# Linear attention in a streaming encoder layer: one 128-column product per decay level for two chunks, outputs with tokens as rows

## The chip, the cores and the metric

The kernel runs on one core of a Trainium2 chip. A core has five engines with a queue of instructions each: PE (matrix products, with its weight loads shown apart as PEld), DVE and ACT (elementwise work), POOL and SP (here mostly issuers of transfers). Each engine works its own queue in order; semaphores make one engine wait for another. Products land in PSUM, a store of eight banks of 512 fp32 columns by 128 partitions; everything else is in SBUF or in DRAM. The metric is the device time of one execution in microseconds (us), and the figure for the kernel before is the median of three runs.

## The reference

One layer of a hybrid encoder for 1024 prompt tokens and 32 sample tokens. The part that the change touches is branch A, a gated linear recurrence with four heads (128 key and 256 value channels per head). Cut to that:

```python
log_a = jax.nn.log_sigmoid((alr @ w_a2 + b_a2).astype(f32)) / GATE_TAU
qb = to_blocks(q, DK_A) * DK_A ** -0.5          # kb, vb, ab likewise

def step(S, inp):
    qi, ki, vi, ai = inp
    b = jnp.cumsum(ai, axis=2)
    decay = jnp.exp(jnp.where(mask, b[:, :, :, None, :] - b[:, :, None, :, :], -jnp.inf))
    scores = jnp.einsum('bhic,bhjc,bhijc->bhij', qi, ki, decay)
    o = (jnp.einsum('bhij,bhjv->bhiv', scores, vi)
         + jnp.einsum('bhic,bhcv->bhiv', qi * jnp.exp(b), S))
    bl = b[:, :, -1]
    S = (jnp.exp(bl)[..., None] * S
         + jnp.einsum('bhjc,bhjv->bhcv', ki * jnp.exp(bl[:, :, None] - b), vi))
    return S, o

s_fin, o = lax.scan(step, s0.astype(f32), (qb, kb, vb, ab))
o = o * lax.rsqrt(jnp.mean(o * o, axis=-1, keepdims=True) + EPS)
o = o.reshape(B, T, V_A) * g_gla.astype(f32)
o = o.astype(q.dtype) * jax.nn.silu(r)
```

Around it stand the input projection `h @ w_in`, a band softmax attention (branch B), the two output projections, a gated convolution feed-forward and an embedding gate, all with normalisations.

## The kernel before

Channels are partitions and tokens are columns through most of the kernel. Dense products run at a precision better than one pass by splitting each operand into a rounded high part and a low remainder (`hi`, `lo`) and adding three products.

The work is staged: input projections, the band attention, the linear attention, the output projections, then the feed-forward and the gate. In the band and linear stages, which are made of small dependent steps, the kernel weaves in dense input projections: `piece()` puts a third of one projection unit on PE (9, 9 or 6 matmuls of 352 columns, lines 808 to 810), `flush()` puts the evacuation of finished units on ACT. The number of units is fixed. PE, DVE and ACT run in the order in which the code issues their instructions (`manual_schedule`); POOL and SP, which issue the transfers, are ordered by the scheduler.

The linear attention takes a head in four segments of 256 tokens (the last has the 32 sample tokens as well, 288 columns), two chunks of 128 tokens each. The main loop `for u in range(16)` does one segment per iteration, head `u // 4`, segment `u % 4`, and prepares the next one beside it.

The decay between two tokens is a product over channels, so the scores cannot be one matrix product. They are built by levels. For level l, with m = 2 to the power l, each block of 2m tokens takes the running sum b of the log gates at its middle as reference: `differences` (DVE, line 1181) subtracts it, `exponentials` (ACT, lines 1201 and 1202; level 6 and the end-of-chunk factors from `refs`, 1190 to 1196) makes decays, `factors` (DVE, 1215, 1209) multiplies the first half of the block by the keys and the second half by the queries, in the same tile `x`. A product of `x` with itself then holds, for that level, the scores between first and second half. `level_products` makes for each of the two chunks and each of levels 1 to 6 one product with the chunk as stationary operand and the 64 second-half columns as moving operand (1242); the diagonal (1227) and level 0 (1233, with `qo`) are made from keys and queries. `score_copies` (DVE, 1264 and 1268) picks the valid elements with byte masks from PSUM into `scores`, which has keys as partitions. `key_turns` and `key_copies` transpose the decayed keys (PE 1249, ACT 1254: tile `kt`), `updates` makes the new states (PE 1283, DVE 1293).

`outputs` makes the output with value channels as partitions, two halves by two chunks, values and state as stationary operand (1306, 1308). For the norm, `squares_a` copies, squares and adds (ACT 1334, 1338, DVE 1340), splits the sum into two parts (1342, 1343), and `sums_a` sums over partitions with a matrix of ones (PE 1348, 1349), so that each partition has the sum of every token. `roots` (ACT 1355 to 1357) and, in the next iteration, `results` (DVE 1365 to 1368) make the inverse root and apply it with the silu gate `sr`.

`decays(h + 1)` is the preparation of the next head in steps: the gate projection (1054), absolute value, exponential and logarithm on ACT (the last is 1060), nine scans on DVE (1064) that give b, the references, and `qo` (1079 to 1082). The loop takes 5, 4 and 3 steps in segments 0, 1 and 2. PSUM has two banks for dense products (`mm`), four single ones (`one`) and one pair (`two`) here.

Of the kernel before, what the change touches and what calls it, by code (L numbers as in the profile page):

```python
# [17 lines left out]
P = 128  # L18
# [95 lines left out]
def emit(tc, a):  # L114
# [584 lines left out]
    masks = tl(gc, [P, 7, 64], U8, tag="masks")  # L699
# [30 lines left out]
    def head_tiles(h):  # L730
        def row(i, scale):
            return lambda ps, s: ac.activation(HA[h][i][:, s], ps, AF.Copy, scale=scale)

        def store(i):
            return lambda t: dma.dma_start(d_kq[i], t)

        box, scale = lambda: HA.setdefault(h, {}), float(P ** -0.5)
        if h:
            kq = [(K0 + h, row("k", 1.0)), (Q0 + h, row("q", scale))]
        else:  # L740
            kq = [(K0 + h, mover(box, "k", 1.0, store(0))), (Q0 + h, mover(box, "q", scale, store(1)))]
# [98 lines left out]
    def band_constants():  # L840
# [8 lines left out]
        for l in range(7):  # L849
            yield  # L850
            m = 1 << l
            po.memset(mf[:, l], 1.0)
            v = mf[:, l].rearrange("p (n m) -> p n m", m=m)
            pat = [[-2 * m, 64 // m], [0, m]]
            po.affine_select(out=v, in_=v, pattern=pat, compare_op=ALU.is_ge, fill=0.0, base=0, channel_multiplier=1)
            pat = [[2 * m, 64 // m], [0, m]]
            po.affine_select(out=v, in_=v, pattern=pat, compare_op=ALU.is_ge, fill=0.0, base=m - 1, channel_multiplier=-1)
        yield
        ve.tensor_copy(masks, mf)
# [183 lines left out]
    def decays(h):  # L1043
        g = HA[h]
        b = g["b"] = tl(gp, [P, T], tag="b", bufs=2) if h else evt()
        ub = b
# [30 lines left out]
        bo, qo = blocks(b, 1), tl(gp, [P, T // 2], tag="qo", bufs=1)  # L1077
# [60 lines left out]
    next(end)  # L1138
    bp.release()

# [3 lines left out]
    scores = [tl(gp, [P, 2, P], tag=f"scores{i}") for i in range(2)]  # L1144
    scores_s = tl(gp, [NS, NS], tag="scores_s")
    for t in scores:
# [25 lines left out]
    def differences(u, ls):  # L1172
# [5 lines left out]
        for l in ls:  # L1178
            m, w = 1 << l, level_width(l, nt)
            bv = blocks(b[:, t0 : t0 + w], m)  # L1180
            ve.tensor_tensor(blocks(x[:, l - 1, :w], m), bv, bv[:, :, m - 1 : m].to_broadcast([P, w // (2 * m), 2 * m]), op=ALU.subtract)

    def exponentials(u, ls):
        g, h, s, t0, nt = seg(u)
        x = X[u]
        for l in ls:
            if l == 7:
                for o in range(0, nt, P):
                    n, w = (t0 + o) // P, min(P, nt - o)
                    ac.activation(x[:, 6, o : o + w], g["b"][:, t0 + o : t0 + o + w], AF.Exp, scale=1.0 / TAU, bias=g["refs"][:, n : n + 1])  # L1190
                ac.activation(x[:, 7, :nt], g["b"][:, t0 : t0 + nt], AF.Exp, scale=-1.0 / TAU)
                continue
            if l == 6:
                for o in range(0, 256, 64):
                    up_, n = o // 64 % 2, (t0 + o) // P
                    ac.activation(x[:, 5, o : o + 64], g["b"][:, t0 + o : t0 + o + 64], AF.Exp, scale=(-1.0 if up_ else 1.0) / TAU,
# [1520 lines left out]
```

## Time and profile before

| | |
|---|---|
| median of 3 runs | 1938.35 us (1938.24 to 1938.88) |
| the profiled execution, its own time | 1942.58 us |
| its span, first to last instruction | 1940.9 us |
| granted PE clock, mean over the span | 0.996 |
| linear attention | about 599 to 912 us of the span |

Each row of a timeline has a start (us from the span's start), a duration in us, the engine, the line, the operation, output tile `<-` inputs, the shape, and how many records are merged. In brackets stands the idle time of the engine before it and what ended it. One fp32 product on PE shows as two records, a transpose or a product of rounded operands as one. Durations on PE overlap their neighbours; the distance between starts does not.

### The profile page before, as it was taken

To read this page: it belongs to the slowest core of one execution; us is meant where nothing else is said; L and a number is where in the kernel's file an instruction comes from. 1 tells how busy PE (TensorE), PEld (TensorE's weight loads), DVE (VectorE), ACT (ScalarE), POOL (GpSimd) and SP (SyncE) were. 2 spreads that over 40 slices of the span, in tenths; PEclk is the share of its full clock that TensorE was granted. 3 is DMA by queue.
4 is the path that set the end of the run, shared out by engine and by line. 5 is a ranking of instruction groups with operands and counts; after the bars stand their busy time and mean duration, and the time that the engine had idled before them with its cause. 6 is when DMAs were issued, how large, how long until landed. Compare 5 with 4: busy or idle time off the path is not lost.

```text
span 1940.9 us, 34940 instructions
## 1 busy us (share of the span) xinstructions
PE 1896.0 (98%) x13960; PEld 1862.0 (96%) x13960; DVE 1258.7 (65%) x2287; ACT 959.0 (49%) x1919; POOL 210.2 (11%) x352
## 2 busy tenths in 40 slices
PE   8999999999999999999999999999999999999996
PEld 8999998998999999999999999999999999999996
DVE  6955544555556776777444685877767766558776
ACT  7544334666666565554233444433334344555555
POOL 0000000000000101001220111111111211000112
PEclk9999999999999999999999999999999999999998
DMA  7223335233315555667844346444354558897746
GB/s 274 85 95 122 100 96 165 74 87 90 93 48 146 142 133 157 166 181 224 299 134 128 105 159 221 159 150 150 113 126 111 124 144 292 273 295 241 242 149 107
DMA packets 111118, 300.91 MB, mean 155 GB/s; under 512 B 12452, under 2 KB 34796, under 8 KB 110316
## 3 DMA queue, kind: packets, MB, share of 16 engines
q1 hardware_dynamic: 81500, 205.95, 33.8%
q0 software_dynamic: 28016, 88.05, 16.9%
q10 hardware_dynamic: 1440, 4.69, 0.6%
q8 instruction: 109, 1.79, 0.4%
q14 instruction: 53, 0.43, 0.1%
HBM read 201.20 MB, written 114.09 MB: 162 GB/s over the span
## 4 chain that ended last, share of the span: by engine, by line
PE 75%; DVE 11%; ACT 7%; DMA 3%; issue 2%; ACTq 0%; SPq 0%; DVEq 0%
PE mm L230 6%; PE mm L232 6%; PE mm L231 6%; PE two L1931 6%; PE two L1932 6%; PE two L1933 6%; PE mm L808 4%; PE two L618 4%; PE two L619 4%; PE two L620 4%; PE mm L810 3%; PE mm L809 3%; PE two L2393 2%; PE two L2392 2%; PE two L2391 2%
## 5 line engine op out<-in xcount | busy, mean ns | idle before, releaser
L808 PE MATMUL mm<-xh,whi 128*128 128x352 f32 x696 | 236.8, 340 | 2.5 <-ACT ev L714 1.8
L810 PE MATMUL mm<-xh,wlo 128*128 128x352 f32 x696 | 225.4, 324 | 0.0
L809 PE MATMUL mm<-xl,whi 128*128 128x352 f32 x696 | 224.6, 323 | 0.0
L2393 PE MATMUL two<-d,wlo 128*128 128x264 f32 x616 | 175.5, 285 | 0.5 <-DVE wlo L2130 0.5
L2392 PE MATMUL two<-d,whi 128*128 128x264 f32 x616 | 174.7, 284 | 0.8 <-DVE d L2081 0.8
L2391 PE MATMUL two<-d,whi 128*128 128x264 f32 x616 | 174.7, 284 | 0.2 <-ACT whi L2129 0.2
L1933 PE MATMUL two<-mh,wlo 128*128 128x264 f32 x576 | 163.3, 285 | 0.2 <-DVE wlo L1922 0.2
L1932 PE MATMUL two<-ml,whi 128*128 128x264 f32 x576 | 162.9, 284 | 0.0
L1931 PE MATMUL two<-mh,whi 128*128 128x264 f32 x576 | 161.4, 285 | 1.5 <-DVE gx L1943 1.5
L808 PEld LDWEIGHTS mm<-xh,whi 128*128 128x128 f32 x696 | 131.3, 189 | 5.0 <-ACT ev L714 2.1
L809 PEld LDWEIGHTS mm<-xl,whi 128*128 128x128 f32 x696 | 131.3, 189 | 0.4
L810 PEld LDWEIGHTS mm<-xh,wlo 128*128 128x128 f32 x696 | 130.5, 188 | 0.0
L2392 PEld LDWEIGHTS two<-d,whi 128*128 128x128 f32 x616 | 115.9, 188 | 1.2 <-DVE d L2081 1.2
L2391 PEld LDWEIGHTS two<-d,whi 128*128 128x128 f32 x616 | 116.5, 189 | 0.5 <-ACT whi L2129 0.5
L2393 PEld LDWEIGHTS two<-d,wlo 128*128 128x128 f32 x616 | 115.5, 188 | 0.9 <-DVE wlo L2130 0.9
L1931 PEld LDWEIGHTS two<-mh,whi 128*128 128x128 f32 x576 | 107.3, 188 | 1.7 <-DVE gx L1943 1.7
L1933 PEld LDWEIGHTS two<-mh,wlo 128*128 128x128 f32 x576 | 108.5, 188 | 0.4 <-DVE wlo L1922 0.4
L1932 PEld LDWEIGHTS two<-ml,whi 128*128 128x128 f32 x576 | 108.4, 188 | 0.0
L944 ACT ACTIVATE s<-s,sm 128x640 f32<-128x640 f32 (+5 forms) x72 | 50.8, 705 | 97.9 <-DVE sm L943 97.9
L619 PE MATMUL two<-tl,whi 128*128 128x264 f32 x320 | 90.8, 284 | 0.0
L618 PE MATMUL two<-th,whi 128*128 128x264 f32 x320 | 90.8, 284 | 0.0
L620 PE MATMUL two<-th,wlo 128*128 128x264 f32 x320 | 90.6, 284 | 0.0
(620 smaller groups left out, 5959.6 us busy)
## 6 DMA issues: line engine op xcount, KB each, us to landing
raw<-in_w_in SPq DMA_DIRECT2D x52, 512.0 KB, 3.7
d_b<-av POOLq DMA_DIRECT2D x33, 528.0 KB, 4.0
d_ws<-in_w_down POOLq DMA_DIRECT2D x24, 704.0 KB, 6.6
uraw<-d_b SPq DMA_DIRECT2D x32, 528.0 KB, 5.2
raw<-in_w_up SPq DMA_DIRECT2D x27, 512.0 KB, 3.6
wraw<-d_ws SPq DMA_DIRECT2D x16, 704.0 KB, 6.4
d_b<-gc POOLq DMA_DIRECT2D x11, 792.0 KB, 6.1
sraw<-in_w_up SPq DMA_DIRECT2D x17, 512.0 KB, 4.6
```

The costliest lines, as they stand in the source:

```text
L618: pe.matmul(ps[:, j, :HC], w[0][:, k], x[0](k, s), start=st, stop=False, skip_group_check=True)
L619: pe.matmul(ps[:, j, :HC], w[0][:, k], x[1](k, s), start=False, stop=False, skip_group_check=True)
L620: pe.matmul(ps[:, j, :HC], w[1][:, k], x[0](k, s), start=False, stop=sp_, skip_group_check=True)
L808: pe.matmul(ps, wh, h[:, k, s], start=(k == 0), stop=False)
L809: pe.matmul(ps, wh, l[:, k, s], start=False, stop=False)
L810: pe.matmul(ps, wl, h[:, k, s], start=False, stop=(k == cnt - 1))
L1931: pe.matmul(ps[:, j, :HC], w[0][:, k], x[0][:, k, s], start=st, stop=False, skip_group_check=True)
L1932: pe.matmul(ps[:, j, :HC], w[0][:, k], x[1][:, k, s], start=False, stop=False, skip_group_check=True)
L1933: pe.matmul(ps[:, j, :HC], w[1][:, k], x[0][:, k, s], start=False, stop=sp_, skip_group_check=True)
L2391: pe.matmul(o, wh, xh_[:, s], start=(k == 0 and p in (0, 4, 5)), stop=False, skip_group_check=True)
L2392: pe.matmul(o, wh, xl_[:, s], start=False, stop=False, skip_group_check=True)
L2393: pe.matmul(o, wl, xh_[:, s], start=False, stop=(k == HD - 1 and p in (3, 4, 6)), skip_group_check=True)
```

## The change

The queries are stored with the two chunks of a pair swapped, in `kq` (`row_swapped`, and four transfers in place of one for head 0), and `decays` makes a second copy of b with the chunks swapped likewise (`both`). `differences` and `factors` then leave in `x` for each level, in the first 128 columns, keys of the first chunk's first halves between queries of the other chunk's second halves, and the reverse in the other 128 columns. One product of these two 128-column parts holds the scores of both chunks: one with keys as partitions, the other with queries as partitions, that is transposed. So `level_products` makes one 128-column product per level where there were two of 64 columns.

The scores of one chunk come out transposed in `sc[:, 0]`: the new `score_turn` transposes them on PE, ACT copies them to `turned`, and DVE puts in level 0. The masks get a second set. `score_copies` runs in two parts, the first (diagonal to level 3) between the level products.

`outputs` now has scores and decayed queries as stationary operands and values and state as moving operands of 256 columns, so tokens are partitions. The norm's sum over channels is then a sum along a row: `squares_a` lets ACT square with an accumulated sum, `roots` works on one number per token and scales the outputs on ACT, and the new `output_turns` transposes them back on PE in the next iteration, where `results` multiplies by the gate. The two products with ones are gone. In PSUM the stage has two `mm` and six `one` banks; unfinished projection units are completed before the change of layout. `decays` has one step more; the loop takes 5, 4, 2 and, in segment 3, two single steps.

How the instructions stand. First PE, in the iteration for head 1, segment 2, from the first product on; dense matmuls are left out at each line of dots. `kq` holds keys and queries, `x` the factors, `vt` the values with tokens as partitions. Before:

```order
L1227 MATMUL one_8102<-kq_6854 128x128 x2
L1233 MATMUL two_8103<-qo_7417,kq_6854 128x64 x2
L1249 MATMUL one_8108<-ident_78,x_7897 128x128 x2
...
L1242 MATMUL two_8103<-x_7897 128x64 x4
...
L1283 MATMUL one_8136<-vt_6855,kt_8134 128x256 x2
L1242 MATMUL two_8103<-x_7897 128x64 x4
...
L1306 MATMUL one_8222<-scores_1112_6731,vt_6855 128x128
L1308 MATMUL one_8222<-x_7897,state_7937 128x128
```

After:

```order
L1325 MATMUL one_8161<-vt_6900,kt_8159 128x256 x2
L1271 MATMUL one_8129<-x_7922 128x128
L1271 MATMUL one_8130<-x_7922 128x128
L1405 MATMUL one_8175<-ident_78,ot_8071 128x128 x4
...
L1279 MATMUL one_8240<-ident_78,scores_1113_6773 128x128
...
L1348 MATMUL one_8257<-state_7961,x_7922 128x256
L1349 MATMUL one_8257<-vt_6900,scores_1113_6773 128x256
L1348 MATMUL one_8257<-state_8164,x_7922 128x256
L1349 MATMUL one_8257<-vt_6900,turned_6775 128x256
```

Four 64-column products became two of 128; the transposes of the previous segment's outputs and of the scores were put in; the last output product reads `turned`.

Next DVE, in the same iteration, from the state updates to the factors of the next segment (`wlo` is the low part of a projection's weights). Before:

```order
L1293 SCALAR_TENSOR_TENSOR state_8141<-state_8139,be_7409,one_8136 128x256
L1264 COPY_PREDICATED scores_1112_6731<-eye_3247,one_8102 128x256
L1268 COPY_PREDICATED scores_1112_6731<-masks_3246,two_8103 128x128
...
L1268 COPY_PREDICATED scores_1112_6731<-masks_3246,two_8103 128x2x64
L1181 TENSOR_TENSOR x_8097<-b_7007 128x256
L1209 TENSOR_TENSOR x_8097<-x_8097,kq_6854 128x576
L1215 TENSOR_TENSOR x_8097<-x_8097,kq_6854 128x288 x4
```

After:

```order
L1311 COPY_PREDICATED scores_1113_6773<-masks_3246,one_8130 128x2x64
L1416 TENSOR_TENSOR sr_7920<-one_8175,sr_7920 128x2x256
L1206 TENSOR_TENSOR x_8123<-both_7448 128x256
L1235 TENSOR_TENSOR x_8123<-x_8123,kq_6899 128x576
L1241 TENSOR_TENSOR x_8123<-x_8123,kq_6899 128x288 x2
L236 TENSOR_TENSOR wlo_8228<-raw_7840,whi_8227 128x512
L1281 COPY_PREDICATED turned_6775<-masks_3246,one_8129 128x64
L1241 TENSOR_TENSOR x_8123<-x_8123,kq_6899 128x288 x2
```

Behind the last level's copy stand now the previous segment's result, the difference, three factors and a weight split, and then the level-0 copy into `turned`.

Last ACT, from the end of segment 1 of head 1 to the key copy of segment 2 (`ev` is the gate of the next head, `kq` the evacuation of a projection, `kt` the key copy). Before:

```order
L1334 ACTIVATE ot_8041<-one_8032 128x2x256
L1338 ACTIVATE sq_1289_8043<-ot_8041 128x2x256
L1342 ACTIVATE y_1290_8046<-sq_1289_8043 128x256
L1060 ACTIVATE ev_7834<-ev_7834 128x1056
L1162 ACTIVATE vt_6855<-one_8064 32x256
L1355 ACTIVATE sq_1289_8043<-one_8080 128x256
...
L732 ACTIVATE kq_7661<-mm_8009 128x352
L1254 ACTIVATE kt_8134<-one_8108 128x256
```

After:

```order
L1383 ACTIVATE ot_8071,sums_8070<-one_8065 128x256 x2
L1070 ACTIVATE ev_7861<-ev_7861 128x1056
L1186 ACTIVATE vt_6900<-one_8089 32x256
L1391 ACTIVATE y_8105<-sums_8070 128x2
L1392 ACTIVATE y_8105<-y_8105 128x2
L1398 ACTIVATE ot_8071<-one_8065,rs_8108 128x256 x2
L740 ACTIVATE kq_7690<-mm_8040 128x32
L740 ACTIVATE kq_7690<-mm_8040 128x128 x2
L740 ACTIVATE kq_7690<-mm_8040 128x64
L1293 ACTIVATE kt_8159<-one_8135 128x256
```

The scaled copies (L1398), which need DVE's `rs`, stand ahead of the evacuation, now in pieces, and of the key copy.

The core of the diff (masks, the swapped query row, and reads of the copy of b in the exponentials are left out):

```diff
     def decays(h):
+        both = g["b"] = tl(gp, [P, 2, T], tag="both", bufs=1)
+        pairs = ((both[:, 0], b), (to[:, :, 1], of[:, :, 0]), (to[:, :, 0], of[:, :, 1]), (both[:, 1, NP:], b[:, NP:]))
+        for i, (t, f) in enumerate(pairs):
+            if i and not h:
+                ve.tensor_copy(t, f)
+            else:
+                ac.activation(t, f, AF.Copy)
+        yield
...
+    repsum((2, 6, 0))
...
     def level_products(u, between):
         for l in range(1, 7):
+            if l == 4:
+                score_copies(u, range(-1, 4))
             if l % 2:
                 between[l // 2]()
-            m = 1 << l
-            for i, (n, o, w) in enumerate(ns):
-                if 2 * m <= w:
-                    xs = x[:, l - 1, o : o + w]
-                    pe.matmul(to(i, l, w), xs, blocks(xs, m)[:, :, m:], start=True, stop=True)
+            pe.matmul(level_bank(u, l), x[:, l - 1, 0:P], x[:, l - 1, P : 2 * P], start=True, stop=True)
...
+    def score_turn(u):
+        r = R[u]
+        ps = ps_one()[:, :P]
+        pe.transpose(ps, r["sc"][:, 0], ident)
+        ac.activation(turned, ps, AF.Copy)
+        ve.copy_predicated(turned.rearrange("p (n s) -> p n s", s=2)[:, :, 1], masks[:, 0, 1], level_bank(u, 0)[:, 64:128])
...
     def outputs(u):
-            for j in range(2):
-                f, d = slice(j * P, (j + 1) * P), ps[:, j * 256 + i * P : j * 256 + (i + 1) * P]
-                pe.matmul(d, g["vt"][:, n, f], r["sc"][:, i], start=True, stop=(n == 0))
-                if n:
-                    pe.matmul(d, S[h, n - 1][:, f], x[:, 7, o : o + w], start=False, stop=True)
+            if n:
+                pe.matmul(d, x[:, 7, P - P * i : 2 * P - P * i], S[h, n - 1], start=True, stop=False)
+            pe.matmul(d, turned if i else r["sc"][:, 1], g["vt"][:, n], start=(n == 0), stop=True)
...
     def squares_a(u):
+        for w, i, ps in parts:
+            ac.activation(t[:w, i], ps, AF.Square, accum_out=v[:w, i : i + 1])
+        ve.tensor_scalar(v, v, 1.0 / 256, EPS, op0=ALU.mult, op1=ALU.add)
...
     def roots(u):
+        ac.activation(y, r["sums"][:, :n], AF.Ln)
         ac.activation(y, y, AF.Exp, scale=-0.5)
+        ve.scalar_tensor_tensor(v, y, -0.5, v, op0=ALU.mult, op1=ALU.mult)
+        ve.tensor_tensor(v, v, y, op=ALU.mult)
+        ve.scalar_tensor_tensor(rs, v, 1.5, y, op0=ALU.add, op1=ALU.mult)
+        for w, i, ps in parts_of(u):
+            ac.activation(r["t"][:w, i], ps, AF.Copy, scale=rs[:w, i : i + 1])
+
+    def output_turns(u):
+                pe.transpose(ps[:, 256 * j + P * i : 256 * j + P * i + P], r["t"][:, i, P * j : P * j + P], ident)
...
     def results(u):
+        ve.tensor_tensor(o[:, :, :256], r["ot"].rearrange("p (j t) -> p j t", t=256), o[:, :, :256], op=ALU.mult)
...
 for u in range(16):
+        def turn_back():
+            if u:
+                output_turns(u - 1)
+            piece()
+
+        level_products(u, (turns, states, turn_back))
...
-        score_copies(u, range(-1, 7))
+        score_copies(u, range(4, 7))
+        if u:
+            results(u - 1)
...
+            factors(u + 1, (7, 1, 2))
+        steps_of(piece, 2)
+        score_turn(u)
+        if u < 15:
+            factors(u + 1, (3, 4, 6))
             exponentials(u + 1, (5,))
-        steps_of(piece, 3)
+        piece()
...
-        sums_a(u)
         roots(u)
...
+    output_turns(15)
     results(15)
```

180 lines of the change are left out of this document (106 added, 74 removed).

## The prediction

> **What bounds the kernel now.** I read the page's totals first, then the table of busy time for the stretch in which the linear attention runs (597 to 912 us), then the timeline of one of its sixteen iterations, engine by engine.
>
> ```profile
> PE 1896.0 (98%) x13960; PEld 1862.0 (96%) x13960; DVE 1258.7 (65%) x2287; ACT 959.0 (49%) x1919; POOL 210.2 (11%) x352
> ...
> 597.00:912.00 315.00, 311.49 (x2134) 298.72 (x2133) 224.23 (x556) 176.90 (x527) 31.48 (x50) 1.00 0.59 163
> ```
>
> The first row is the whole span with PE busy for 98% of it. The columns of the second are the stretch, its length, and the busy time of PE, PEld, DVE, ACT and POOL, then the granted clock (1.00). PE is idle for 3.5 us of 315; DVE has 29% to spare, ACT 44%. Dense projections fill every hole that the attention leaves on PE, and their number does not change. So in this stretch a microsecond of PE work removed is a microsecond gained, as long as no new wait stands where the old work stood.
>
> The profile's durations overlap on PE, so I price PE work by the distance of starts. This is iteration 6 (head 1, segment 2), PE:
>
> ```profile
> 713.44 0.28 PE L1348 MATMUL one<-y,onesHr 128*128 128x256 f32 x1
> 713.67 0.39 PE L1349 MATMUL one<-y,onesHr 128*128 128x256 f32 x1
> 713.89 0.61 PE L1227 MATMUL one<-kq 128*128 128x128 f32 x4
> 714.34 0.56 PE L1233 MATMUL two<-qo,kq 128*128 128x64 f32 x4
> 714.73 0.39 PE L1249 MATMUL one<-ident,x 128*128 128x128 f32 x2
> 714.87 0.41 PE L808 MATMUL mm<-xh,whi 128*128 128x352 f32 x1
> 715.12 0.32 PE L809 MATMUL mm<-xl,whi 128*128 128x352 f32 x1
> ...
> 716.41 1.00 PE L1242 MATMUL two<-x 128*128 128x64 f32 x8
> 717.22 0.41 PE L808 MATMUL mm<-xh,whi 128*128 128x352 f32 x1
> 717.46 0.33 PE L809 MATMUL mm<-xl,whi 128*128 128x352 f32 x1
> ...
> 718.76 1.03 PE L1283 MATMUL one<-vt,kt 128*128 128x256 f32 x4
> 719.62 1.00 PE L1242 MATMUL two<-x 128*128 128x64 f32 x8
> ...
> 726.28 0.38 PE L1306 MATMUL one<-scores,vt 128*128 128x128 f32 x2
> ...
> 728.23 0.32 PE L809 MATMUL mm<-xl,whi 128*128 128x352 f32 x1
> ```
>
> A dense matmul of 352 columns takes 0.161 us (eight from 715.12 to 716.41). An fp32 product is two records. Two products of 128 columns (four records, L1227) go by in 0.45 us, 0.112 us a record. Four products of 64 columns (eight records, L1242) take 717.46 - 716.41 - 0.16 = 0.89 us up to the second dense matmul: 0.111 a record. So 64 columns cost what 128 cost; something of fixed length, the weight load by the look of it, sets the pace. 256 columns (L1283) cost 0.86 / 4 = 0.215 a record. A transpose (L1249) is one record: (715.12 - 714.73 - 0.16) / 2 = 0.115.
>
> **The change, part by part, on PE, per iteration.** Each line is the work that goes or comes, by these prices.
> - Levels 1 to 6: twelve products of 64 columns become six of 128, twelve records fewer: 12 x 0.112 = 1.34 us less.
> - Outputs: sixteen records of 128 columns (726.28 to 728.23, less 0.16: 1.79) become eight of 256 (8 x 0.215 = 1.72): 0.07 less.
> - The two norm products L1348 and L1349 go. At the dense rate 256 columns are 0.117 each, 0.23 for both; from 713.44 to 713.89 they hold PE for 0.45. I take the middle, 0.34, and keep both ends (16 x 0.11 = 1.8 us either way).
> - Five transposes come (one for the turned scores, four for the outputs): 5 x 0.115 = 0.57 more.
> - Products for the 32 sample tokens change form in four iterations: wider moving operands, fewer instructions. I put them at zero, 0.3 us an iteration either way.
>
> Sum: 1.34 + 0.07 + 0.34 - 0.57 = 1.18 us, over sixteen iterations 18.9 us less PE work. Nothing on PE covers this or is covered by it: it is the path.
>
> The level products hold most of this, and there a rule of the Trainium skill speaks against the change. In "TensorE: Matmul & The Clock Gate", section "Back-to-back issue gap", the gap of an isolated matmul grows with its columns: about 60 cycles up to 64 columns, 134 at 128. By it one product of 128 columns would cost a little more than two of 64, and the 1.34 us would be about nothing. The rows above differ (0.112 against 0.111 a record), and the same section says that weight loads in a stream set a floor, so I go by the rows; the sum by the rule is the last of the rivals.
>
> **What the other engines have to do in time.** The outputs of the second chunk now need a chain that did not exist: last level copied into the scores (DVE), scores turned (PE), moved to SBUF (ACT), level 0 patched in (DVE), then the product. For its length, DVE in the same iteration, and the sample copies of iteration 7:
>
> ```profile
> 714.16 2.75 DVE L1064 TENSOR_TENSOR_SCAN b<-b,ev 128x128 f32<-128x128 f32 x9 [0.22 <-ACT ev L1060]
> ...
> 720.52 0.99 DVE L1293 SCALAR_TENSOR_TENSOR state<-state,be,one 128x256 f32<-128x256 f32 x2
> 721.43 0.44 DVE L1264 COPY_PREDICATED scores<-eye,one 128x256 f32<-128x256 uint8 x1
> 722.52 2.60 DVE L1268 COPY_PREDICATED scores<-masks,two 128x128 f32<-128x128 uint8 x7 [0.65 <-PE two L1242]
> 725.03 0.42 DVE L1181 TENSOR_TENSOR x<-b 128x256 f32<-128x256 f32 x1
> 725.36 0.75 DVE L1209 TENSOR_TENSOR x<-x,kq 128x576 f32<-128x576 f32 x1
> 726.03 1.90 DVE L1215 TENSOR_TENSOR x<-x,kq 128x288 f32<-128x288 f32 x5
> 727.84 0.69 DVE L236 TENSOR_TENSOR wlo<-raw,whi 128x512 fp32r<-128x512 f32 x1
> ...
> 746.37 0.98 DVE L1275 COPY_PREDICATED scores_s<-masks,one 32x16 f32<-32x16 uint8 x5
> ```
>
> PE's new timetable, from the iteration's first product: opening 1.07 (713.89 to 715.12 less 0.16), nine dense 1.45, two levels 0.45, nine dense 1.45, updates 0.86 (ends at 5.3), two levels 0.45, four transposes 0.46, six dense 0.97, two levels 0.45 (level 6 ends at 7.6), eighteen dense 2.90, the turn 0.12 (10.6), six dense 0.97, three output products of 0.43: at 12.9 us the turned scores are wanted.
>
> DVE: states from 5.5 (0.23 us behind PE, as 722.52 is behind the end of the products) for 0.91; diagonal 0.44; level 0, 64 elements wide, 0.25 (between the 0.2 of L1275 and the 0.36 of L1268); three levels at 0.36 (2.51 / 7), to 8.2; three more to 9.3. Then the new result multiply, 512 elements, at 0.67 like L1209: 9.9; difference 0.33, factors 0.67 and 2 x 0.36, weight split 0.6, to 12.3; the level-0 patch 0.25 and 0.1 to 0.2 of signalling: 12.7 against 12.9. It just fits; queued behind the patch are the other factors, which are wanted an iteration later. I allow 0.15 us in each of twelve iterations: 1.8 us. In segment 3 DVE has 1.1 us of sample copies and 0.7 (like L1209) of the next head's qo more ahead of the patch, and starts the last copies 0.9 later, while PE's sample products move the need by 1.3 only: 12.7 + 2.7 = 15.4 against 14.2. Three iterations wait 1.1 us each: 3.3 us. (The sixteenth has no next segment to prepare.)
>
> Next, ACT around the end of segment 1 of head 1:
>
> ```profile
> 710.98 0.60 ACT L1334 ACTIVATE ot<-one 128x512 f32<-128x512 f32 x1 [1.19 <-PE one L1308]
> ...
> 713.06 1.07 ACT L1060 ACTIVATE ev<-ev 128x1056 f32<-128x1056 f32 x1
> ...
> 715.81 0.38 ACT L1254 ACTIVATE kt<-one 128x256 f32<-128x256 f32 x1
> ```
>
> Before, ACT does its part of the norm and goes on to the key copy `kt` at 4.8 us behind its first look at the outputs. Now its scaled copies (L1398 after) wait for three small DVE instructions, and in segment 1 these stand behind the nine scans (2.75 us). ACT: two squares with their sums, no row has that form, between 0.8 (two copies like `kt`) and 1.3 (as much as the copy and the square now gone), I take 1.2; logarithm 1.07; scans 2.75; three small operations 0.5; two scaled copies 0.75; four pieces of the query row instead of one, 1.0; `kt` 0.38: 7.7 us. PE wants `kt` after 2.7 us of fill (fifteen dense matmuls and two transposes) and 4.4 of the next iteration (its opening, nine dense, two levels, nine dense), 7.1. Behind ACT's wait stand the evacuation of a projection bank and `kt`, and PE's update waits for that. Where the fill is longer (segments 0 and 2, up to 24 dense matmuls) it is hidden. I count 1.0 us for the stage. That DVE loses some 2 us of norm arithmetic in each iteration gains nothing by itself: it is not the bound.
>
> The beginning has no slack:
>
> ```profile
> 598.74 0.71 DVE L1082 TENSOR_TENSOR qo<-qo,kq 128x528 f32<-128x528 f32 x1 [6.75 <-DMA kq<-d_kq]
> 598.76 0.52 PEld L1227 LDWEIGHTS one<-kq 128*128 128x128 f32 x4 [0.57 <-ACT vt L1162]
> ```
>
> The first products start the moment `kq` lands. It now comes by four transfers on SP's queue, and ACT's copy of b (1.07, like L1060) goes ahead of the exponentials. Between 0 and 2.5 us; I take 1.0. At the end, the turned outputs of the sixteenth segment stand behind two and a half pieces of dense work, about 3.9 us, and their chain (squares of three parts 1.8, four splits on ACT at the 0.44 of L1264's width 1.8, roots and three scaled copies 2.1) is 5.7: 2 us of wait.
>
> The extra mask building in the band phase is on POOL, idle there, and one more DVE copy; the query row's eleven pieces are 1.7 us of ACT per head with 44% of it free: zero. They lose their cover only if ACT becomes late, which is the point above.
>
> Waits: 1.8 + 3.3 + 1.0 + 1.0 + 2.0 = 9.1 us. Net 18.9 - 9.1 = 9.8 us less: the profiled execution's 1942.58 us would be 1932.8. It stands 4.2 us above the median of the runs, 1938.35, so the median should come to 1928.5; I say 1928.
>
> **Rivals.**
> - No wait shows: DVE and ACT run ahead where I have them just late. The spare 29% and 44% speak for it; the missing slack at the start and the segment-3 sum speak against it. 1938.35 - 18.9 = 1919.5, with the upper end of the norm products 1918.
> - The waits eat the gain: the patch comes 0.65 us later in fifteen iterations than I have it (0.65 x 15 = 9.8), by signalling between four engines for instance. 1938. My margin of 0.2 us speaks for it.
> - Slower: the predicated copies. They now read PSUM with a stride and write two blocks at unlike offsets, a form without a row. If each of the six took twice 0.36 us, the patch would be 2.2 us later, 15 x 2.2 = 32 us, less the 0.2 of margin each time: about 1957. It turns to a loss from 0.12 us more per copy. Against it: L1268's seven already write with strides of 2 to 64 elements and take the same 0.36.
> - Products of 128 columns cost two of 64. Then 12 x 0.112 x 16 = 21.5 us of the saving are gone: 18.9 - 21.5 - 9.1 = -11.7, 1950. This is the way of the skill's rule above; the trace does not bear it out, so it gets 0.03.
>
> **Chances.** Forecast, 1920 to 1934: 0.55. No wait shows, below 1920: 0.16. Gain eaten: 0.12. Slower copies 0.11, dear products 0.03, another loss on ACT's side 0.03. This kernel's measurement can tell about 0.2% (3.9 us) from no change, so faster is 0.71, the same 0.12, slower 0.17. The range 1916 to 1943 leaves out the losses and the tip of the best case, about 0.19; the forecast's own is 1920 to 1934.
>
> **What would show it.** Six level products per iteration as records of 128 columns at 0.112 us, 192 in all; four transposes in the middle of each iteration. PE's waits in the stage about 7 to 10 us, largest at the product that reads the turned scores in segment 3, on DVE; some on the key copy after segment 1; one at the start and one before the last turns. If the level records stand 0.22 apart, the price of columns was wrong. If PE waits over 1.2 us in every iteration, the chain was.

## The result, and the profile after

The changed kernel took 1925.88 us (median of 6 runs, 1925.19 to 1929.69) beside 1938.62 for the kernel before (6 runs): a ratio of 0.9936, with a 95% interval of 0.9923 to 0.9949, so 9.9 to 14.9 us less. The forecast was 1928, with 9.8 us less on the profiled execution.

The table of busy time by stretch, first of the kernel before and then of the changed one, each cut at the start of the stage's first product and the end of its last dense one (columns as in the prediction: stretch, length, busy time of PE, PEld, DVE, ACT and POOL, granted clock):

```profile
598.78:923.43 324.65, 320.82 (x2187) 307.77 (x2187) 231.41 (x564) 180.76 (x531) 37.28 (x53) 1.00 0.60 164
```

```profile
597.29:904.80 307.51, 301.91 (x1908) 280.91 (x1906) 203.14 (x569) 179.89 (x627) 35.61 (x57) 1.00 0.62 173
```

The stage is 17.1 us shorter. PE's busy time fell by 18.9, its idle time rose from 3.8 to 5.6; PE is still the bound. DVE is the engine whose share moved: 71% before, 66% now. Part of the 17.1 is a shift, not a gain: the same view of the first dense line alone (PE and PEld only) shows 360 products ahead of the stage before and 363 now. There are three such lines, so nine dense products, 9 x 0.161 = 1.45 us, are done earlier: `while fill["now"]` ahead of the new bank layout completes an open unit. Like for like the stage lost 15.7 us. The time fell by 12.7, so some 3 us of the stage's gain do not show in it (see "Again").

```profile
0.00:598.78 598.78, 121.08 (x360) 67.92 (x360) 1.00 0.36 112
```

```profile
0.00:597.29 597.29, 122.17 (x363) 68.60 (x363) 1.00 0.36 113
```

PE's list of waits in the stage, before and after (what waited, for what: us in total, times, the longest):

```profile
PE mm L808 <- DVE ev L790: 1.4, 2, 0.8
...
PE mm L808 <- ACT ev L714: 0.3, 1, 0.3
```

```profile
PE one L1349 <- DVE turned L1281: 1.3, 3, 0.5
PE one L1264 <- DVE qo L1101: 1.1, 1, 1.1
PE one L1325 <- ACT kt L1293: 1.0, 2, 0.8
PE mm L818 <- ACT kq L732: 0.7, 1, 0.7
PE mm L818 <- ACT ev L714: 0.4, 1, 0.4
PE one L1185 <- ACT ev L714: 0.4, 1, 0.4
PE one L1405 <- ACT ot L1398: 0.2, 1, 0.2
```

Before, five rows make 3.7 us (1.4, 0.9, 0.8, 0.3, 0.3; the first and the last are shown); after, seven make 5.1. The four waits that the prediction named are all there: the turned scores, the first products, the key copy, the last turns. They sum to 3.6 us; 9.1 were forecast. Since some waits of before are gone, PE's waits in all rose by no more than 1.4 us.

One group of four level records in the changed kernel, with the dense products behind it:

```profile
677.45 0.61 PE L1271 MATMUL one<-x 128*128 128x128 f32 x4
677.81 0.41 PE L818 MATMUL mm<-xh,whi 128*128 128x352 f32 x1
678.06 0.32 PE L819 MATMUL mm<-xl,whi 128*128 128x352 f32 x1
```

678.06 - 677.45 - 0.16 = 0.45 us for four records of 128 columns, as priced; the eight of 64 columns took 0.89.

### The profile page after: what moved, and what is told of

Same layout as the page of the kernel before. It is cut to its first block, busy times and chain, and to the rows that moved or that the text cites. A ratio compares the mean times of both kernels' runs of the same rounds, so it can differ in the third digit from the quotient of the medians.

```text
span 1925.0 us, 34527 instructions
## 1 busy us (share of the span) xinstructions
PE 1879.9 (98%) x13688; PEld 1839.1 (96%) x13688; DVE 1231.7 (64%) x2295; ACT 955.9 (50%) x2012; POOL 214.0 (11%) x376
## 4 chain that ended last, share of the span: by engine, by line
PE 57%; DVE 5%; ACT 4%; DMA 3%; issue 1%; SPq 0%; DVEq 0%; ACTq 0%
PE two L2003 6%; PE two L2005 6%; PE two L2004 6%; PE mm L230 5%; PE mm L232 5%; PE mm L231 5%; PE two L2465 3%; PE two L2464 3%; PE two L2463 3%; PE mm L818 3%; PE mm L820 3%; PE mm L819 3%; DMA hn<-d_hn 1%; PE one L1271 1%; PE one L1325 1%
## 5 line engine op out<-in xcount | busy, mean ns | idle before, releaser
L1993 ACT ACTIVATE whi<-ws 128x512 fp32r<-128x512 f32 x72 | 45.2, 631 | 92.2 <-PE two L2004 68.6
```

## The experiments

The stage (here from the start of its first product to the start of its last dense one) turned out the sharper instrument: two profiles of one kernel agree in it within 0.1 us, while whole runs scatter by 2 us and more.

| run | time, us | ratio to before | 95% interval | stage, us |
|---|---|---|---|---|
| before, first and second profile | 1938.6, 1939.6 | 1, 0.9995 | 0.9982 to 1.0008 (second) | 324.3, 324.2 |
| changed, first and second profile | 1925.9, 1928.6 | 0.9936, 0.9930 | 0.9914 to 0.9946 (second) | 307.2, 307.1 |
| split_levels | 1946.4 | 1.0035 | 1.0022 to 1.0049 | 324.0 |
| rows_only | 1943.3 | 1.0023 | 1.0014 to 1.0032 | 323.7 |
| copies_twice | 1948.9 | 1.0053 | 1.0039 to 1.0067 | 331.1 |
| merged0 | 1927.6 | 0.9943 | 0.9929 to 0.9958 | 307.4 |
| merged0b | 1925.0 | 0.9916 | 0.9902 to 0.9931 | 305.0 |
| merged0c | 1923.3 | 0.9908 | 0.9893 to 0.9924 | 302.6 |
| cols_out | 1962.8 | 1.0110 | 1.0093 to 1.0127 | 343.6 |
| cols_out2 | 1939.7 | 1.0000 | 0.9991 to 1.0009 | 319.6 |
| cols_merged | 1941.5 | 1.0011 | 1.0002 to 1.0020 | 320.8 |
| cols_out3 | 1950.3 | 1.0050 | 1.0037 to 1.0064 | 329.1 |

All rows but the first have 363 dense products of each line ahead of the stage, so among them the stages compare directly; against before, 1.45 us are to be added. In some profiles PE's granted clock stands at half for 3.4 us at a time within the stage: once in rows_only and in copies_twice, twice in cols_merged, four times in cols_out3, longer in cols_out, never in the others. Each such stretch makes the stage some 1.5 us longer (estimated in the last section).

**What a column costs (split_levels).**

```diff
-            pe.matmul(level_bank(u, l), x[:, l - 1, 0:P], x[:, l - 1, P : 2 * P], start=True, stop=True)
+            for e in (0, 64):
+                pe.matmul(level_bank(u, l)[:, e : e + 64], x[:, l - 1, 0:P], x[:, l - 1, P + e : P + e + 64], start=True, stop=True)
```

> The changed kernel, but each level product of 128 columns is made as two of 64 columns from the same operands: twelve records more per iteration, all else as it was. If a record costs 0.112 us whether it has 64 or 128 columns (the prediction's rows), the run takes 16 x 12 x 0.112 = 21.5 us more than the changed kernel, less up to 1.3 us of waits that the longer PE work covers: 1945 to 1948, with the level records 0.112 apart. If the price goes by columns (the rule on the gap of isolated matmuls in the Trainium skill, which was a rival), the halves cost half each: 1926 to 1929, records about 0.06 apart.

The stage came to 324.0, 16.9 us more, and the whole merging gain is gone. The same group, now eight records on line 1272:

```profile
678.20 1.00 PE L1272 MATMUL one<-x 128*128 128x64 f32 x8
679.00 0.41 PE L818 MATMUL mm<-xh,whi 128*128 128x352 f32 x1
679.25 0.32 PE L819 MATMUL mm<-xl,whi 128*128 128x352 f32 x1
```

679.25 - 678.20 - 0.16 = 0.89 us: 0.111 a record, half the columns for the same price. So the gain is in the number of records, and the rival that 128 columns cost two of 64 falls. (The Trainium skill, "TensorE: Matmul & The Clock Gate", section "Back-to-back issue gap", has about 60 cycles for 64 columns and 134 for 128 for an isolated matmul; this stream does not follow that table.) The 16.9 is less than the 21.5 of 192 records at 0.112. PE's waits in this run are 3.2 us against 5.1, which hides 1.9. The rest is the price: counted from each start to the next, idle time left out, the level records of the two chunks (those of the sample tokens left out) hold PE for 22.7 us in the changed kernel (192 of them) and for 41.9 here (384), so a record more costs 0.10 on average, a little less than in the group shown.

**The other half alone (rows_only).** The kernel before, with outputs, norm, transposes back and banks of the changed one. Core of the edit, beside the new `squares_a`, `roots`, `output_turns` and `results` and the two banks `lo` and `hi`:

```diff
-            for j in range(2):
...
-                pe.matmul(d, g["vt"][:, n, f], r["sc"][:, i], start=True, stop=(n == 0))
-                if n:
-                    pe.matmul(d, S[h, n - 1][:, f], x[:, 7, o : o + w], start=False, stop=True)
...
+            if n:
+                pe.matmul(d, x[:, 7, P * i : P * i + P], S[h, n - 1], start=True, stop=False)
+            pe.matmul(d, r["sc"][:, i], g["vt"][:, n], start=(n == 0), stop=True)
```

> The kernel before with one half of the change alone: outputs with tokens as rows, their norm, the four transposes back, and the banks of the changed kernel; the level products stay at two of 64 columns per level and nothing is turned. By the prices on PE an iteration loses 0.07 us on the outputs and 0.45 on the norm products and gains 0.46 for four transposes: 1 us less in sixteen iterations, and about 1 us of new waits (key copy, last turns) against it: the time of before within 2 us, 1937 to 1940. If the relief of DVE (some 1.5 us less norm work in each iteration) or the cheaper output form is what made the kernel faster, 1934 or less. If ACT's wait for the three small DVE operations costs at each segment, 1942 or more.

By time it is 0.23% slower (0.14 to 0.32), more than the 2 us of the first case. The stage is 323.7 + 1.45 - 324.25 = 0.9 us longer. That is less than what one stretch at half clock costs it:

```profile
655.20:658.60 3.40, 3.40 (x12) 2.78 (x10) 0.61 (x1) 3.40 (x17) 0.00 (x0) 0.50 0.76 191
```

Without that stretch the stage would be some 0.6 us shorter than before (an estimate). PE's waits in it are 3.2 us against 3.7, 1.0 of them for the key copy; so the third case, ACT's wait at each segment, is not what costs. Its profiled span, 1940.3 us, is that of before (1940.9 and 1939.8). Where the timed runs lose the other 3 us stays open; its three slowest (1945.9 to 1948.7) are the ones with the lowest mean clock, 0.994. By itself, then, this half gains nothing.

**How much room the chain to the turned scores has (copies_twice).**

```diff
-            ve.copy_predicated(to, masks[:, l].rearrange("p c (n m) -> p c n m", m=m), of)
+            for again in range(2):
+                ve.copy_predicated(to, masks[:, l].rearrange("p c (n m) -> p c n m", m=m), of)
```

> The changed kernel with each of the six level copies on DVE made twice (same result): about 2.1 us more DVE work per iteration ahead of the turned scores. The prediction's chain had 0.2 us of margin in each of fifteen iterations: 15 x 1.9 = 28 us more, 1954. The trace of the changed kernel has between 0 and 1.9 us from the end of the level-0 copy to the product that reads it, and 0.1 to 1.4 from the last level copy to the transpose; from these, iteration by iteration, the waits come to 17 to 24 us: 1943 to 1950. If the copies are not on the path at all: 1926 to 1928.

The time is above the changed kernel's by 1.17% of the kernel before (1.0053 against 0.9936), 22.7 us; the stage is 23.9 longer. PE's waits:

```profile
PE one L1279 <- DVE scores L1312: 13.4, 12, 1.8
PE one L1350 <- DVE turned L1281: 5.6, 6, 1.9
```

19.0 us at the two places, 12 and 6 times, where the changed kernel has 1.3; of the other 6.2 us, some 1.5 are the stretch at half clock. So the chain is on the path, as the prediction said, and what kept that rival away was the copies' price (they are 0.33 us each in the profile) and the room: 2.0 us more work on DVE per iteration became 17.7 / 16 = 1.1 us more wait, so the room is some 0.9 us per iteration and not 0.2.

**Level 0 merged as well (merged0, merged0b, merged0c).** Even keys are copied between the odd queries once per head (`qo` gets 1056 columns); one 128-column product replaces the two of L1264, and the level-0 copy into `turned` goes:

```diff
-            pe.matmul(to(i, 0, w), k[:, n * P : n * P + w], qo[:, m * 64 : m * 64 + w // 2], start=True, stop=True)
+        pe.matmul(level_bank(u, 0), qo[:, t0 : t0 + P], qo[:, t0 + P : t0 + 2 * P], start=True, stop=True)
...
-        ve.copy_predicated(turned.rearrange("p (n s) -> p n s", s=2)[:, :, 1], masks[:, 0, 1], level_bank(u, 0)[:, 64:128])
```

> The changed kernel with level 0 treated as the other levels: even keys are copied once per head between the odd queries (ACT), one 128-column product replaces two of 64, and the level-0 copy into the turned scores goes (level 0 is in the scores before they are turned). The gate rows are loaded after the previous result is stored, into one buffer, to make room. Two records of 0.112 us fewer per iteration are 3.6 us; the wait for the turned scores (1.3 us in the trace) becomes less or goes: 1921 to 1923 beside 1925.9. The rival: the copy of keys makes the first products later by what it takes (0.6 us or more) and the later load holds up the weight loads behind it on the same queue, so that 1925 to 1928 comes out.

No gain at first. The wait for the turned scores was gone from PE's list, but my way of making room (one buffer for the gate rows, loaded behind the previous result) brought another, once, in the last iteration. PE's list and DVE's, from 820 us on:

```profile
PE mm L818 <- DVE ev L800: 3.0, 1, 3.0
...
DVE sr L1419 <- DMA sr<-d_sr: 3.1, 1, 3.1
```

merged0b loads the last gate rows at the start of that iteration, into the free `x` buffer:

```diff
+        if u == 15:
+            gates(u)
```

> The kernel with level 0 merged, mended in one place: in the last iteration the gate rows are loaded at its start, into a free buffer. Its wait of 3.0 us there (DVE for the gate rows, PE behind it) goes: 3 us less than merged0 and 3 to 4 us less than the changed kernel, 1921 to 1923 at a before of 1938.6. If the merged level 0 has no worth of its own, it stays level with the changed kernel.

305.0: 2.3 us less than merged0, and 2.1 less than the changed kernel. That is the two records fewer, and not all of them: PE's waits sum to 5.1 us as in the changed kernel, since the 1.3 for the turned scores went and the others grew. merged0c moves `roots` in segment 1 ahead of the last scans:

```diff
+        if s == 1:
+            roots(u)
         steps_of(lambda: next(chain, None), n // 2)
```

> As merged0b, and in segment 1 the roots of the norm come ahead of the last scans of the next head, so that ACT's scaled copies and the key copy behind them need not wait for the scans. The wait for the key copy (1.3 us in merged0, 1.0 in the changed kernel) goes: 1 us less than merged0b. If the scans were not what ACT waited for, the wait stays and the time with it.

302.6. PE's wait for the key copy fell from 1.3 to 0.4:

```profile
PE one L1324 <- ACT kt L1295: 0.4, 1, 0.4
```

So the scans were what ACT's scaled copies, and `kt` behind them, waited for, as the prediction had it; the stage gained more (2.4 us) than that wait (0.9). All five runs of merged0c (1922.7 to 1924.1) lie below all twelve of the changed kernel (1925.2 and up): it is faster than both, by 0.92% against before, and has the lowest median of all versions.

**The level half alone (cols_out, cols_out2, cols_merged, cols_out3).** The changed kernel with the outputs and the norm of before:

```diff
-            pe.matmul(d, turned if i else r["sc"][:, 1], g["vt"][:, n], start=(n == 0), stop=True)
...
+            for j in range(2):
...
+                pe.matmul(d, g["vt"][:, n, f], turned if i else r["sc"][:, 1], start=True, stop=(n == 0))
...
-                output_turns(u - 1)
...
+        sums_a(u)
         roots(u)
```

> The changed kernel with the other half of the change undone: one level product per level, scores turned, but outputs with channels as rows and the norm of before (products with ones, no transposes back; its rounded squares lie in a projection buffer to make room, and the gate rows have one buffer). By the prices on PE the stage hardly moves: in an iteration the norm products cost 0.46 us more, the four transposes 0.48 less, the outputs 0.1 more, some 1 us more in all; the run with the rows alone gave the stage of before within 1 us, too. If that is all, 1926 to 1929 and a stage of 307 to 309 us. The rival: DVE has some 1.3 us more norm work in each iteration, and the level-0 copy stands behind it with 0 to 1.9 us of margin, 1.0 in the mean; then the wait for the turned scores grows by 0.3 us and more in each iteration, 6 to 15 us in all: a stage of 313 to 322 us, 1933 to 1942.

This was a miss of the experiment, not of a theory: the rounded squares took a buffer in the ring that the decays load into, and PE waited for that load.

```profile
PE one L1064 <- DMA ev<-d_alr: 23.0, 3, 9.6
```

cols_out2 puts the squares into the finished part of `x` and the rounded ones into a tile of their own (against cols_out):

```diff
-        yt = tl(ev, [P, T], F32R, tag="ev", bufs=evb[0])
-        y = r["y"] = [yt[:, 288 * i : 288 * i + nt] for i in range(2)]
+        y = r["y"] = [tl(gp, [P, 288], F32R, tag=f"y{i}")[:, :nt] for i in range(2)]
...
-        sq = r["sq"] = tl(gp, [P, 2, 288], tag="sq2")
+        sq = r["sq"] = X[u][:, 2:4]
```

> As cols_out (one product per level and scores turned, but outputs with channels as rows and the norm of before), with the rounded squares no longer in a projection buffer: in cols_out that buffer held up the load of the decays' input, and PE waited 23 us for it in segments 3, which hid what was asked. Without these 23 us the stage of cols_out is 320.6, against 307.2 with tokens as rows; its waits at the turn and at the turned scores are 6.6 us there against 1.3. So, if the norm work on DVE is what delays the chain: a stage of 314 to 321 us and 1933 to 1940. If the 13 us were an after-effect of the held buffer: 307 to 309 us and 1926 to 1929.

The stage is 319.6, 12.4 us more than with tokens as rows, and the time is that of before (1.0000, within 0.09%). The table by stretch, and PE's first waits:

```profile
598.80:918.80 320.00, 303.75 (x2004) 286.09 (x2002) 230.75 (x581) 192.41 (x587) 37.23 (x53) 1.00 0.61 167
```

```profile
PE one L1279 <- DVE scores L1311: 7.0, 6, 1.6
PE one L1390 <- ACT y L1384: 1.6, 2, 1.0
PE one L1348 <- DVE turned L1281: 1.6, 4, 0.7
```

PE is busy 303.75 us, hardly more than the 301.91 of the changed kernel; it idles 16.2 us against 5.6, and 7.3 of these 10.6 us more stand at the transpose of the scores and at the product that reads them. DVE's own waits say why, first in the changed kernel, then here:

```profile
DVE state L1335 <- PE one L1325: 25.9, 12, 4.3
...
DVE state L1333 <- PE one L1325: 11.5, 4, 4.3
```

```profile
DVE x L1407 <- ACT x L1399: 19.0, 9, 4.5
...
DVE state L1335 <- PE one L1325: 1.7, 3, 0.6
...
DVE state L1333 <- PE one L1325: 1.3, 2, 0.9
```

In the changed kernel DVE reaches the state updates ahead of PE in all sixteen iterations and waits 37.4 us there: that is its lead, and the chain to the turned scores runs on it. With the norm of before DVE has 27.6 us more work (230.75 against 203.14) and stands 19 us behind ACT's last root ahead of the state updates, where 3.0 us of the lead are left. The other runs fit: rows_only, which turns no scores, has 35.6 us of this wait (22.3 and 13.3), the kernel before 4.4 (3.5 and 0.9). So it is the half with tokens as rows that makes the lead. Whether the work or the standing takes it away, no run separates. ACT also stood 5.5 us for the store of the previous outputs, since this version has one buffer `ot`; cols_merged has none of that wait and is no faster, so the buffer is at most a small part of it.

cols_merged takes the level-0 copy out of the chain as well:

> cols_out2 with level 0 merged as in merged0, which takes the level-0 copy out of the chain behind the turned scores. If DVE's queue in front of that copy is what makes the waits of cols_out2, most of the waits at the product that reads the turned scores go, those at the transpose itself stay: a stage 4 to 8 us shorter than cols_out2's (two records fewer per iteration are 2 to 3.6 us of it). If the order with tokens as rows has no worth beyond that, it comes level with merged0b (a stage of 305 us); if it has, it stays 5 us or more above.

320.8, 15.7 above merged0b; two stretches at half clock, some 3 us, are in it. The wait at the product shrank (0.5 us), the one at the transpose grew:

```profile
PE one L1282 <- DVE scores L1310: 10.6, 8, 2.1
```

cols_out3 moves the norm's last operations off the head of the next iteration, three to the end of their own and one behind the score copies (against cols_out2):

```diff
-        if u:
-            results(u - 1)
         loads(u)
...
         roots(u)
+        norms(u)
```

> As cols_out2, but the norm's last operations no longer stand at the head of the next iteration, ahead of its states and scores: the three of them that need no gate (1.5 us on DVE) come at the end of their own iteration, and the product with the gate (0.7 us) stands behind the score copies, where the changed kernel has it. If the place of this work in DVE's queue made the waits of cols_out2 (7.0 us at the transpose of the scores, 1.6 at the product), these fall to 1 or 2 us, the stage goes from 319.6 to 311 to 313 us, and the time to 1931 to 1934. If the amount of work on DVE and ACT did, whatever its order, the stage stays at 317 to 320 us and the time at that of before.

Neither came: 329.1. DVE now stood for ACT's last root 24.0 us, 11 times, in place of 19.0, since the operations that need it were put just behind it; and some 6 of the 9.5 us came from the clock (last section). Whether some other order would rescue outputs with channels as rows was not tried.

**Again (before_again, after_again).** Both kernels as they are.

> The kernel before, profiled once more, to see how far two profiles of one kernel differ by stage. In the first pair of profiles the attention stage (first product to last dense one) was 324.3 us before and 307.2 after, while the part behind it was 2.6 us longer after, with a wait of 2.5 us for a DMA some 300 us behind the stage, in code that the change does not touch. If that is chance, the two parts of this profile differ from the first one's by as much; if before never has such waits, they belong to the change.

> The changed kernel once more: 0.992 to 0.995 of before by time; a stage of 306 to 308 us; the waits behind the stage between 0 and 3 us if they are chance, near 3 again if they belong to the change.

The stage repeats to 0.1 us, and so do its waits. What lies behind it, from its end to the end of the span, was 1017.5 and 1018.1 us before, 1020.2 and 1020.0 after, and 1017.5 to 1022.8 in the ten others. What lies ahead of it scattered more: the second profile of the changed kernel reached the stage at 604.1 us, the first at 597.3; in the second PE's clock stood at half for 6.8 us from 306 us on and for 3.4 from 511 on. The first profile has such a stretch behind the stage, 3.4 us from 1228 us on, the second has none there and is as long. A loss of 2 us behind the stage that belongs to the change is possible, but other kernels with the same stage layout lack it (merged0b 1017.5); it stays open.

## Why the prediction was right, point by point

- **PE work, 18.9 us.** PE's busy time fell by 18.9, of which 1.45 is the shift of nine dense products: 17.5. The price by records held (0.45 and 0.89 us for the two groups, split_levels), if not to the last digit: counted the same way, the level records of the two chunks held PE for 41.6 us before and 22.7 after, 18.9 less where 21.5 were priced. For the half with tokens as rows (outputs, norm products, four transposes) the prediction's own lines sum to 0.8 us more work; rows_only's stage was 0.9 longer with its half-clock stretch and some 0.6 shorter without, next to nothing either way.
- **Waits, 9.1 us.** This is the term that was mis-sized: 3.6 measured. The key copy (1.0 forecast, 1.0 found) had the right size, and the place in part: 0.8 of it came behind segment 1 of head 2, the other 0.2 behind segment 0 of head 0, and head 1, for which it was worked out, has none. The start (1.0 and 1.1) had the right size and one of its two causes: the transfers of `kq` did no harm, since its products started at 597.30 us without a wait. PE waited for `qo` (L1264), whose exponential came up on ACT at 597.60, and ACT had been busy without a pause since 591.2, with the copy of b (1.07 us) first. "I allow 0.15 us in each of twelve iterations" and 1.1 in segments 3 (5.1 in all) became 1.3 in three waits. The forecast was worked out for iteration 6, and there it was near: the level-0 copy ended 13.26 us after the first product (12.7 forecast), PE stood 0.24 us. But most other iterations have turns of values (L1185) or more dense work on PE ahead of the outputs, or an earlier copy; in eleven of the sixteen that copy ended 0.4 to 1.9 us before PE came to it (from the timelines, iteration by iteration), and in two more it was just in time.
- **Who is last in segment 3.** The prediction put the 1.1 us on DVE's queue. It was right. Iteration 7, PE's, ACT's and DVE's rows of the changed kernel:

```profile
736.20 0.27 PE L1279 MATMUL one<-ident,scores 128*128 128x128 f32 x1
...
739.26 0.70 PE L1349 MATMUL one<-vt,turned 128*128 128x256 f32 x2 [0.53 <-DVE turned L1281]
...
735.90 1.06 ACT L1222 ACTIVATE x<-both,refs 128x64 f32<-128x64 f32 x4
736.86 0.64 ACT L1099 ACTIVATE qo<-qo 128x528 f32<-128x528 f32 x1
737.39 0.62 ACT L235 ACTIVATE whi<-raw 128x512 fp32r<-128x512 f32 x1
737.91 0.26 ACT L1280 ACTIVATE turned<-one 128x128 f32<-128x128 f32 x1
...
738.31 0.68 DVE L236 TENSOR_TENSOR wlo<-raw,whi 128x512 fp32r<-128x512 f32 x1
738.92 0.29 DVE L1281 COPY_PREDICATED turned<-masks,one 128x64 f32<-128x64 uint8 x1
```

The transpose was done at 736.47; ACT took it up at 737.91, behind the exponentials, the exponent of `qo` for the next head and a weight split, and was done with it at 738.17. DVE, which worked without a pause, came to its level-0 copy only at 738.92, behind its own weight split. So ACT's copy was late too, but DVE's queue alone set the wait; in all sixteen iterations the level-0 copy started without idle time on DVE, and ACT's copy had ended before. The sizes were off on both sides: the copy ended 16.7 us after the first product (15.4 forecast), and PE came 16.2 us after it (739.26 - 0.53 - 722.49), not 14.2, so the wait was 0.53 and not 1.1 (15.4 - 14.2 is 1.2, a slip of rounding in the sum). merged0 took DVE's copy out, and the wait went.
- **The end, 2.0 us.** 0.2 found. The transposes do not wait for all three scaled copies: the first started at 891.86, 0.53 us after ACT's copies began (891.33), with 0.65 of their 1.18 us to go.
- **The sum, and luck in it.** Work 17.5 instead of 18.9 and waits and gaps up by 1.8 instead of 9.1 make 15.7 us less in the stage, not 9.8. That the median came to 1925.9, 2 us from the 1928 of the forecast, is also due to the 3 us that the time lost outside the stage, for which the prediction had no term. So the direction and the main term were understood; the closeness was in part luck.
- **Rivals.** "No wait shows" (1919.5) was 6.4 us too low: the waits, the smaller gain of the levels and the loss outside the stage. "The waits eat the gain" did not come, though copies_twice shows that 2 us more of DVE's work per iteration do more than that (1948.9). "The predicated copies": 0.33 us each, not twice 0.36 (and 15 x 2.2 is 33, not 32). "128 columns cost two of 64": refuted by split_levels.
- **What the prediction missed.** It wrote: "That DVE loses some 2 us of norm arithmetic in each iteration gains nothing by itself: it is not the bound." rows_only agrees with the words "by itself". But without that relief the level half gains nothing either (cols_out2, 1.0000): the two halves are worth +0.23% and 0.00% alone and -0.64% together. The forecast was right since it took both as given, not since it saw this.

## What to carry to other kernels

Where short products stand in a stream and each record costs the same from 64 to 128 columns, count records, not columns. Before such a change, ask how far the engine that prepares its operands runs ahead of PE, and read that from the waits of that engine on PE: 37 us of them were the reserve that the new chain ran on, and the half of the change that lightened DVE paid only through it. In a kernel whose whole time scatters by more than the step that is studied, compare the stage: it repeated here to 0.1 us. Look at the granted clock within it first: one stretch at half clock was more than all that rows_only seemed to lose.

## What was not expected of the hardware

PE's granted clock can fall after only a short gap in PE's work. In cols_out3, segment 3 of head 1 waited 0.93 us for the turned scores up to 750.8 us and then ran the products of the 32 sample tokens; from 753.0 us on the clock stood at half for 3.4 us, although dense work filled PE from 753.3 on. The table by stretch (the first number behind the five busy times is the clock), and PE's rows:

```profile
752.00:753.00 1.00, 1.00 (x7) 0.88 (x7) 0.00 (x0) 0.60 (x1) 0.50 (x1) 1.00 0.00 0
753.00:754.00 1.00, 1.00 (x5) 1.00 (x5) 0.45 (x2) 0.00 (x0) 0.00 (x0) 0.51 0.76 113
755.00:756.00 1.00, 1.00 (x5) 1.00 (x4) 0.46 (x1) 0.47 (x3) 0.00 (x0) 0.50 0.88 347
757.00:758.00 1.00, 1.00 (x9) 1.00 (x8) 0.40 (x1) 0.00 (x0) 0.38 (x1) 1.00 0.35 66
```

```profile
754.05 0.49 PE L820 MATMUL mm<-xh,wlo 128*128 128x352 f32 x1
754.35 0.49 PE L818 MATMUL mm<-xh,whi 128*128 128x352 f32 x1
```

Dense products stand 0.29 us apart there in place of 0.161, so such a stretch loses about 3.4 x (1 - 0.161 / 0.29) = 1.5 us (an estimate from these rows). cols_out3's stage has four of them (from 753.0, 872.5, 893.0 and 920.3 us), some 6 us of the 9.5 by which it is longer than cols_out2's; PE's idle time makes the other 3.8. The Trainium skill ("TensorE: Matmul & The Clock Gate", section "What's actually happening") has the half rate and a window of about 3.4 us, and both agree; it lets the clock fall after an idle window, and here the gaps ahead of a fall were shorter: 0.93 us at 753.0, 1.15 in rows_only at 655.2, 0.53 in cols_merged at 748.8. What decides stays open. The length of the gap alone does not: merged0 kept 1.00 after its gap of 3.0 us. The small products of the sample tokens do not either: the falls at 872.5 here and at 646.4 in cols_merged had none in the 3.4 us ahead of them, but gaps of 2.1 and 2.0 us. The changed kernel and the one before keep 1.00 through the stage, so a wait that grows towards a microsecond can cost more than itself.
